# Attention of the prompt: score tiles over two PSUM banks, and GpSimd in the split of q and k and in the squares of the output

## The chip, the core and the metric

The kernel runs on one core of a Trainium2 chip. The core has five engines with an instruction queue each: PE (matrix products, with its weight loads shown as PEld), DVE (vector), ACT (scalar and activation functions), POOL (GpSimd) and SP (here it only issues DMAs). They work on SBUF, 128 partitions wide, and on PSUM, which has eight banks of 512 fp32 columns per partition; products land in PSUM. The metric is the device time of one execution in microseconds, as the median of several runs.

## The reference

One inference step of a decoder with two layers: gated linear attention, then differential attention, each followed by an MLP and layer norms. It treats a prompt of 1024 tokens after 16 meta tokens, and eight running sequences with one new token each. The change lies in the differential attention of the prompt, 8 heads, each with two maps of 64 dimensions and values of 128:

```python
def diff_core(q, k, v, q_pos, k_pos, lam):
    s = jnp.einsum('bqhmd,bkhmd->bhmqk', q, k).astype(F32) * (DIFF_DH ** -0.5)
    mask = k_pos[None, :] <= q_pos[:, None]
    s = jnp.where(mask, s, -jnp.inf)
    p = jax.nn.softmax(s, axis=-1)
    a = p[:, :, 0] - lam * p[:, :, 1]
    return jnp.einsum('bhqk,bkhe->bqhe', a, v.astype(F32))

def diff_output(o, g_sub, lam_init, w_out, dtype):
    B, T = o.shape[:2]
    o = rms_norm(o, g_sub) * (1.0 - lam_init)
    return o.reshape(B, T, DIFF_HEADS * DIFF_DV).astype(dtype) @ w_out
```

So per head: scores of both maps, causal mask, two softmaxes, their weighted difference times the values, and a root-mean-square norm over the 128 values of a head, for which the squares of the output are summed.

## The kernel before

The kernel is one long function, `hybrid_step`. Instructions are written in program order in a tile framework. A planner puts them on the engines in an order of its own, worked out with modelled times, and inserts the waits; each engine then runs its queue strictly in that order. Tiles come from pools: a pool with `bufs=3` has three places for a name, and a fourth tile of that name waits until the first is free. PSUM is shared out for the whole kernel as three banks `mm` (products), three `ax` (transposes and small things) and two `sm` (long accumulations).

Products of fp32 accuracy are made of fp32r parts: `split` (L159 to L161) casts a tile to its high part on ACT (L160) and subtracts that from the tile on DVE (L161), which leaves the low part.

The attention stage (L1036 to L1198) runs over 8 heads and, in each, over 8 query tiles t of 128 rows.

- `prep(h)` (L1054) loads k, q and v of a head from DRAM, transposes k and q on PE through `ax` banks, four blocks of 128 at a time (L1077, L1082, L1087), and splits them into the tiles XH and XL (L160, L161). It writes into one half of XH and XL, head h + 1 while head h uses the other half. For heads 1 to 7 nine DMAs on POOL's queue (`move`, L1093 to L1099) then spread and copy parts over partitions, so that one product of 128 rows does the work of two of 64. Three of the moves (L1094 and twice L1099) overwrite what an earlier one reads, and wait on POOL for its landing. `prep(h + 1)` stands in program order ahead of the first tile of head h.
- `tile_(h, t, ...)` (L1102) has W = 16 + 128 (t + 1) keys. It cuts W into 1, 2 or 3 pieces of at most 512, and per map and piece makes the scores in one `mm` bank (L1117 to L1119 for head 0, L1121 and L1122 for the others). One DVE instruction (L1125, in the profile a custom operation and a read of its accumulator) scales the piece by -0.125, adds the mask, writes it to SBUF (`as`) and leaves the running minimum of the row. The first piece of a row starts from a constant, the later ones from the minimum so far. Then ACT makes the exponentials and their sums (L1127), DVE the weights (L1129, L1130) and the difference of the maps (L1131), PE transposes it (L1140), ACT copies that to SBUF (L1142), and PE multiplies by the values into the output bank `po`, an `sm` bank (L1145).
- After every fourth tile ACT copies the output bank to Y (L1180), squares it in place (L1181), and DVE sums the squares (L1182).
- After every second head `o_norm` scales the heads on POOL (a power in L1156, a multiply of 128x2048 in L1157). The last head is scaled in two parts on DVE, and `o_fm` transposes the result into XH and XL for the output projection.

The mask tile `cm` (`cmask`) has 448 columns: zeros, and the causal triangle in the last 128.

Of the kernel before, what the change touches and what calls it, by code (L numbers as in the profile page):

```python
# [88 lines left out]
def hybrid_step(ctx, tc, A, dbg=None, upto=9):  # L89
# [10 lines left out]
    mm = ctx.enter_context(tc.tile_pool(name="mm", bufs=3, space=PSUM))  # L100
    ax = ctx.enter_context(tc.tile_pool(name="ax", bufs=3, space=PSUM))
    sm = ctx.enter_context(tc.tile_pool(name="sm", bufs=2, space=PSUM))

    def mmt():
        return mm.tile([P, 512], F32, name="mmt")

    def axt():
        return ax.tile([P, 512], F32, name="axt")

    def smt():  # L110
        return sm.tile([P, 512], F32, name="smt")

    def cload(name, pool=cp):
        a, b = CCOL[name]
# [939 lines left out]
    def prep(h):  # L1054
# [22 lines left out]
        TE.transpose(ps[:, :NM], km, ident[:NM, :NM])  # L1077
        split(kh_[:, :NM], kl_[:, :NM], ps[:, :NM])
        for c in range(2):
            ps = axt()  # L1080
            for i in range(4):
                TE.transpose(ps[:, i * P : (i + 1) * P], kx[:, 4 * c + i, :], ident)  # L1082
            cs = slice(NM + 512 * c, NM + 512 * c + 512)
            split(kh_[:, cs], kl_[:, cs], ps)
            ps = axt()
            for i in range(4):
                TE.transpose(ps[:, i * P : (i + 1) * P], qx[:, 4 * c + i, :], ident)  # L1087
            cs = slice(512 * c, 512 * c + 512)
            split(qh_[:, cs], ql_[:, cs], ps)
        if h == 0:  # L1090
            return vm, vx, kh_, qh_, ql_, kl_
        move = nc.gpsimd.dma_start
# [8 lines left out]

    def tile_(h, t, out, vm, vx, k2, q2, ql2, kl_):  # L1102
        W = NM + P * (t + 1)
        nch = -(-W // 512)
        step = -(-W // nch // 16) * 16
        cuts = [(x, min(x + step, W)) for x in range(0, W, step)]
        sc_ = scp.tile([P, 2, NM + T], F32, name="as")
        st = a3.tile([P, 2, 2], F32, name="ast")
        mns, neg = st[:, 0, :], st[:, 1, :]
        l = ls[:, t, h, :]  # L1110
        ts_ = slice(t * P, (t + 1) * P)
        for m in range(2):
            r = slice(64 * m, 64 * m + 64)
            for ci, (x, y) in enumerate(cuts):
                ps = mmt()[:, : y - x]
                if h == 0:
                    TE.matmul(ps, q2[r, ts_], k2[r, x:y], start=True, stop=False)  # L1117
                    TE.matmul(ps, q2[r, ts_], kl_[r, x:y], start=False, stop=False)
                    TE.matmul(ps, ql2[r, ts_], k2[r, x:y], start=False, stop=True)  # L1119
                else:  # L1120
                    TE.matmul(ps, q2[m][:, ts_], k2[m][:, x:y], start=True, stop=False)  # L1121
                    TE.matmul(ps, ql2[m][:, ts_], k2[m][:, x:y], start=False, stop=True)  # L1122
                w = y - x
                mk = cm[:, CW - w :] if y == W else cm[:, 0:1].broadcast_to([P, w])
                V.tensor_tensor_reduce(sc_[:, m, x:y], ps, mk, -0.125, -NEG if ci == 0 else mns[:, m : m + 1], ALU.add, ALU.min, mns[:, m : m + 1])  # L1125
        for m in range(2):
            S.activation(sc_[:, m, :W], sc_[:, m, :W], AF.Exp, bias=mns[:, m : m + 1], scale=-1.0, accum_out=l[:, m : m + 1])  # L1127
# [3 lines left out]
        V.scalar_tensor_tensor(sc_[:, 0, :W], sc_[:, 1, :W], neg[:, 0:1], sc_[:, 0, :W], ALU.mult, ALU.add)  # L1131

        keys = [(0, vm)] + [(NM + j * P, vx[:, j, :]) for j in range(t + 1)]
        ats = []
        for j0 in range(0, t + 2, 4):
            n = min(4, t + 2 - j0)
            ps = axt()
            for j in range(n):
                x = keys[j0 + j][0]
                TE.transpose(ps[:, j * P : (j + 1) * P], sc_[:, 0, x : x + P], ident)  # L1140
            at = a3.tile([P, 4, P], F32, name="aT")
            S.copy(at[:, :n, :].rearrange("p j q -> p (j q)"), ps[:, : n * P])  # L1142
            ats += [at[:, j, :] for j in range(n)]
        for j, (at, (x, v)) in enumerate(zip(ats, keys)):
            TE.matmul(out, at, v, start=j == 0, stop=j == t + 1)  # L1145
# [23 lines left out]
    for h in range(8):  # L1169
        head = nxt  # L1170
        for n, t in enumerate((3, 2, 1, 0, 7, 6, 5, 4) if h == 7 else (7, 1, 5, 3, 6, 0, 4, 2)):
# [6 lines left out]
            if n % 4 == 3:  # L1178
                ts = (slice(0, 4), slice(4, 8))[n // 4] if h == 7 else slice(t % 2, 8, 2)
                S.copy(Yd[:, ts, h], po.rearrange("p (t e) -> p t e", e=P))  # L1180
# [139 lines left out]
```

## Time and profile before

| | |
|---|---|
| median of 3 runs | 2976.41 us (2976.1 to 2979.01) |
| profiled execution, whole | 2971.24 us |
| its span in the profile | 2969.5 us |
| granted TensorE clock, mean | 0.989 |
| PE busy | 2871.7 us, 97% |
| PE weight loads busy | 2321.0 us, 78% |
| DVE busy | 1578.4 us, 53% |
| ACT busy | 944.4 us, 32% |
| POOL busy | 846.2 us, 28% |
| chain that ended last, by engine | PE 79%, DVE 8%, DMA 7% |

The profile is of one execution. Busy times are unions over the engine's instructions; records of matmuls overlap, so a busy PE isn't a PE at its peak. Averages over the span mix stages with different limits: the first two thirds and the last quarter are weight products, and the attention of the prompt lies between, from about 1823 us to about 2090 us of the span. In a row of a timeline, the first number is the start, the second the duration, and a bracket at the end tells how long the engine was idle before and what ended that. In a row of a group, the count follows the shapes; then come busy microseconds and the mean of one in nanoseconds, and after that idle time before.

### The profile page before, as it was taken

To read this page: it belongs to the slowest core of one execution; us is meant where nothing else is said; L and a number is where in the kernel's file an instruction comes from. 1 tells how busy PE (TensorE), PEld (TensorE's weight loads), DVE (VectorE), ACT (ScalarE), POOL (GpSimd) and SP (SyncE) were. 2 spreads that over 40 slices of the span, in tenths; PEclk is the share of its full clock that TensorE was granted. 3 is DMA by queue.
4 is the path that set the end of the run, shared out by engine and by line. 5 is a ranking of instruction groups with operands and counts; after the bars stand their busy time and mean duration, and the time that the engine had idled before them with its cause. 6 is when DMAs were issued, how large, how long until landed. Compare 5 with 4: busy or idle time off the path is not lost.

```text
span 2969.5 us, 50730 instructions
## 1 busy us (share of the span) xinstructions
PE 2871.7 (97%) x19476; PEld 2321.0 (78%) x19476; DVE 1578.4 (53%) x2713; ACT 944.4 (32%) x1970; POOL 846.2 (28%) x605
## 2 busy tenths in 40 slices
PE   8999999999999999999989999999999999999998
PEld 5766668987767667666788887888998889888886
DVE  2563544468777766776777722889452212211115
ACT  2343344152122122122321113778242232223322
POOL 1322122234333433433323320223312222222224
PEclk9999999999999999999999999999999999999999
DMA  8667551525798887989588988564411111111111
GB/s 275 192 205 239 177 176 38 180 84 161 272 322 302 284 312 266 348 290 316 197 270 292 355 292 228 108 124 106 167 33 56 50 42 34 57 43 47 37 38 65
DMA packets 265730, 525.55 MB, mean 177 GB/s; under 512 B 30528, under 2 KB 162368, under 8 KB 261392
## 3 DMA queue, kind: packets, MB, share of 16 engines
q1 hardware_dynamic: 260448, 505.71, 50.9%
q0 software_dynamic: 5040, 16.61, 2.8%
q8 instruction: 153, 2.51, 0.4%
q14 instruction: 89, 0.73, 0.1%
HBM read 479.65 MB, written 25.99 MB: 170 GB/s over the span
## 4 chain that ended last, share of the span: by engine, by line
PE 79%; DVE 8%; DMA 7%; issue 2%; POOL 1%; ACT 1%; SPq 1%; DVEq 0%; POOLq 0%; ACTq 0%
PE mmt L164 22%; PE mmt L166 22%; PE mmt L165 22%; PE smt L776 4%; PE smt L1145 2%; DVE pg L735 1%; DVE as L1125 1%; DMA pg<-in_cache_v 1%; PE smt L953 1%; DMA swt<-in_mlp_w 1%; PE smt L417 1%; PE axt L1140 1%; DVE sc L736 1%; PE axt L891 1%; DVE as L1131 1%
## 5 line engine op out<-in xcount | busy, mean ns | idle before, releaser
L152 POOL TENSOR_TENSOR wlo<-raw,whi 128x512 fp32r<-128x512 f32 x384 | 528.7, 1393 | 1375.9 <-ACT whi L151 1220.9
L164 PE MATMUL mmt<-XH,whi 128*128 128x512 f32 (+1 forms) x1536 | 555.6, 362 | 5.8 <-DVE HL L161 5.8
L166 PE MATMUL mmt<-XH,wlo 128*128 128x512 f32 (+1 forms) x1536 | 554.4, 361 | 0.0
L165 PE MATMUL mmt<-XL,whi 128*128 128x512 f32 (+1 forms) x1536 | 553.6, 361 | 0.0
L151 ACT CAST whi<-raw 128x512 fp32r<-128x512 f32 x384 | 227.5, 619 | 931.1 <-PE mmt L166 492.6
L164 PE MATMUL mmt<-whi,XH 128*128 128x256 f32 x1536 | 440.5, 288 | 7.4 <-ACT Y L561 3.9
L165 PE MATMUL mmt<-wlo,XH 128*128 128x256 f32 x1536 | 437.7, 286 | 0.8 <-POOL wlo L152 0.8
L166 PE MATMUL mmt<-whi,XL 128*128 128x256 f32 x1536 | 437.3, 285 | 0.0
L164 PE MATMUL mmt<-whi,HH 128*128 128x512 f32 x1024 | 411.2, 402 | 1.4 <-DVE Y L962 1.4
L166 PE MATMUL mmt<-whi,HL 128*128 128x512 f32 x1024 | 407.7, 398 | 0.0
L165 PE MATMUL mmt<-wlo,HH 128*128 128x512 f32 x1024 | 407.4, 398 | 0.0
L736 DVE TENSOR_REDUCE sc<-pg 128x16 f32<-128x1024 f32 x256 | 308.9, 1213 | 86.5 <-POOL pg L735 83.8
L962 DVE TENSOR_TENSOR Y<-Y,mmt 128x512 f32<-128x512 f32 x256 | 174.9, 684 | 326.9 <-PE mmt L166 326.3
L164 PEld LDWEIGHTS mmt<-XH,whi 128*128 128x128 f32 x1536 | 290.0, 189 | 47.5 <-issue 10.1
L165 PEld LDWEIGHTS mmt<-XL,whi 128*128 128x128 f32 x1536 | 289.7, 189 | 46.7 <-issue 15.6
L166 PEld LDWEIGHTS mmt<-XH,wlo 128*128 128x128 f32 x1536 | 289.9, 189 | 44.7 <-issue 12.6
L164 PEld LDWEIGHTS mmt<-whi,XH 128*128 128x128 f32 x1536 | 290.5, 189 | 32.8 <-issue 22.9
L165 PEld LDWEIGHTS mmt<-wlo,XH 128*128 128x128 f32 x1536 | 290.8, 189 | 17.4 <-issue 15.4
L166 PEld LDWEIGHTS mmt<-whi,XL 128*128 128x128 f32 x1536 | 290.7, 190 | 10.3 <-issue 9.7
L735 DVE TENSOR_TENSOR pg<-pg,qb 128x1024 f32<-128x1024 f32 x192 | 264.5, 1383 | 36.3 <-DMA pg<-in_cache_k 29.6
L161 DVE TENSOR_TENSOR HL<-mmt,HH 128x344 fp32r<-128x344 f32 (+1 forms) x160 | 93.1, 583 | 351.9 <-ACT HH L160 351.8
L164 PEld LDWEIGHTS mmt<-whi,HH 128*128 128x128 f32 x1024 | 192.9, 188 | 74.4 <-issue 16.5
(371 smaller groups left out, 3623.2 us busy)
## 6 DMA issues: line engine op xcount, KB each, us to landing
pg<-in_cache_k SPq DMA_DIRECT2D x256, 512.0 KB
pg<-in_cache_v SPq DMA_DIRECT2D x256, 512.0 KB
raw<-in_mlp_w SPq DMA_DIRECT2D x256, 256.0 KB
swt<-in_mlp_w SPq DMA_DIRECT2D x32, 1024.0 KB
raw<-in_gla_w_in SPq DMA_DIRECT2D x48, 256.0 KB
swt<-in_gla_w_in SPq DMA_DIRECT2D x12, 1024.0 KB
swt<-in_diff_w_in SPq DMA_DIRECT2D x12, 1024.0 KB
raw<-in_diff_w_in SPq DMA_DIRECT2D x48, 256.0 KB
```

The source lines that it names most:

```text
L151: S.copy(hi[:, c], raw)
L152: G.tensor_tensor(lo[:, c], raw, hi[:, c].bitcast(F32), op=ALU.subtract)
L161: return eng.tensor_tensor(lo, src, hi.bitcast(F32), op=ALU.subtract)
L164: TE.matmul(ps, ah, bh, start=first, stop=False)
L165: TE.matmul(ps, ah, bl, start=False, stop=False)
L166: TE.matmul(ps, al, bh, start=False, stop=last)
L417: TE.matmul(ps[o : o + TS, :], lhs[:, k + i, :], t[:, i, c * 512 : (c + 1) * 512], start=k == 0, stop=k == nk - 2)
L735: eng.tensor_tensor(pg, pg, qb, op=ALU.mult)
L736: V.tensor_reduce(sc[:, n, :], pg.rearrange("p (h d) -> p h d", d=64), op=ALU.add, axis=AX.X)
L776: TE.matmul(acc[i * TS : i * TS + 16, :256], w[r, n, :], pg[r, i * 256 : (i + 1) * 256], start=n == 0, stop=n == NPG)
L962: steps_v.append(V.tensor_tensor(yv, yv, ps, op=ALU.add).ins)
L1145: TE.matmul(out, at, v, start=j == 0, stop=j == t + 1)
```

## The change

Three things are changed in the stage.

1. The PSUM banks are shared out anew for the stage: two buffers `sc` of two banks each for scores, three `ax`, and one `sm` in place of two. Before and after the stage the old shares hold. A row of W scores is cut into 1, 2 or 4 equal pieces of at most 512; up to two pieces lie in the two banks of one `sc` buffer, and one L1125 takes both. The mask tile grows to 912 columns for that.
2. For heads 1 to 7, k and q are not split by ACT and DVE out of PSUM. ACT copies the transposed 128x512 to SBUF (`fm`, two buffers), GpSimd copies it to the high part and subtracts for the low part. Head 0, and the 16 meta columns of k, are split as before.
3. The squares of the output are made by GpSimd from Y in SBUF into a tile `o2`, in place of ACT's square in the bank; DVE sums `o2`.

```diff
@@
+    banks = {}
+
+    def psum(**bufs):
+        if banks:
+            banks.pop("all").close()
+        e = banks["all"] = ExitStack()
+        for n, b in bufs.items():
+            banks[n] = e.enter_context(tc.tile_pool(name=n, bufs=b, space=PSUM))
+
+    ctx.callback(lambda: banks["all"].close())
+    psum(mm=3, ax=3, sm=2)
...
     de.close()
+    psum(sc=2, ax=3, sm=1)
...
+    a4 = e.enter_context(tc.tile_pool(name="a4", bufs=2))
     scp = e.enter_context(tc.tile_pool(name="scp", bufs=5))
-    CW = 448
+    CW = 912
...
+            for x, hi, lo, o in ((kx, kh_, kl_, NM), (qx, qh_, ql_, 0)):
+                ps = axt()
+                for i in range(4):
+                    TE.transpose(ps[:, i * P : (i + 1) * P], x[:, 4 * c + i, :], ident)
+                cs = slice(o + 512 * c, o + 512 * c + 512)
+                if h == 0:
+                    split(hi[:, cs], lo[:, cs], ps)
+                    continue
+
+                f = a4.tile([P, 512], F32, name="fm")
+                S.copy(f, ps)
+                G.tensor_copy(hi[:, cs], f)
+                G.tensor_tensor(lo[:, cs], f, hi[:, cs].bitcast(F32), op=ALU.subtract)
...
-        nch = -(-W // 512)
-        step = -(-W // nch // 16) * 16
-        cuts = [(x, min(x + step, W)) for x in range(0, W, step)]
+        nch = (1, 2, 4)[(W > 512) + (W > 1024)]
+        n = W // nch
...
-            for ci, (x, y) in enumerate(cuts):
-                ps = mmt()[:, : y - x]
...
-                V.tensor_tensor_reduce(sc_[:, m, x:y], ps, mk, -0.125, -NEG if ci == 0 else mns[:, m : m + 1], ALU.add, ALU.min, mns[:, m : m + 1])
+            for c in range(0, nch, 2):
+                k = min(nch, 2)
+                pss = banks["sc"].tile([P, 2, 512], F32, name="sct")[:, :k, :n]
+                for i in range(k):
+                    x, ps = (c + i) * n, pss[:, i, :]
+                    y = x + n
...
+                w, x = k * n, c * n
+                mk = cm[:, CW - w :] if x + w == W else cm[:, 0:1].broadcast_to([P, w])
+                f = lambda a: a.rearrange("p (i n) -> p i n", i=k)
+                V.tensor_tensor_reduce(f(sc_[:, m, x : x + w]), pss, f(mk), -0.125, -NEG if c == 0 else mns[:, m : m + 1], ALU.add, ALU.min, mns[:, m : m + 1])
...
-                S.activation(po, po, AF.Square)
-                V.tensor_reduce(oss[:, ts, h], po.rearrange("p (t e) -> p t e", e=P), op=ALU.add, axis=AX.X)
+                o2 = a4.tile([P, 4, P], F32, name="o2")
+                G.tensor_tensor(o2, Yd[:, ts, h], Yd[:, ts, h], op=ALU.mult)
+                V.tensor_reduce(oss[:, ts, h], o2, op=ALU.add, axis=AX.X)
...
     e.close()
+    psum(mm=3, ax=3, sm=2)
```

The functions `mmt`, `axt` and `smt` take their tiles from the share that holds at the time.

More of the change, by code (lines that the diff above doesn't have):

```diff
@@ L99, in hybrid_step @@
     wrp = ctx.enter_context(tc.tile_pool(name="wrp", bufs=2))
-    mm = ctx.enter_context(tc.tile_pool(name="mm", bufs=3, space=PSUM))
-    ax = ctx.enter_context(tc.tile_pool(name="ax", bufs=3, space=PSUM))
-    sm = ctx.enter_context(tc.tile_pool(name="sm", bufs=2, space=PSUM))
+    banks = {}
[7 more added lines that the diff above has]
+    psum(mm=3, ax=3, sm=2)
     def mmt():
-        return mm.tile([P, 512], F32, name="mmt")
+        return banks["mm"].tile([P, 512], F32, name="mmt")
     def axt():
-        return ax.tile([P, 512], F32, name="axt")
+        return banks["ax"].tile([P, 512], F32, name="axt")
     def smt():
-        return sm.tile([P, 512], F32, name="smt")
+        return banks["sm"].tile([P, 512], F32, name="smt")
     def cload(name, pool=cp):
```

26 lines of the change are left out of this document (7 added, 19 removed).

## The prediction

> **What bounds the kernel now.** I read the page first for the span, then the whole change lies in one stage, attention of the prompt, so I cut that stage by head in the table of windows (each row from one head's first score matmul to the next one's), and after it the chain of waits, the list of waits, and the timeline around head switches.
>
> ```profile
> span 2969.5 us, 50730 instructions
> ```
>
> ```profile
> core 0: us, PE busy (x) PEld busy (x) DVE busy (x) ACT busy (x) POOL busy (x), PEclk, DMA share, GB/s
> 1860.00:1888.00 28.00, 26.54 (x202) 24.55 (x200) 25.73 (x91) 22.93 (x57) 4.58 (x9) 1.00 0.63 134
> 1888.00:1921.00 33.00, 29.08 (x209) 25.97 (x209) 29.25 (x91) 22.44 (x56) 11.14 (x11) 0.98 0.61 128
> 1921.00:1953.00 32.00, 29.60 (x196) 27.05 (x197) 24.67 (x81) 21.39 (x51) 4.58 (x9) 0.86 0.64 125
> 1953.00:1987.00 34.00, 29.99 (x221) 27.36 (x220) 28.11 (x98) 27.06 (x67) 8.80 (x11) 0.96 0.55 115
> 1987.00:2014.00 27.00, 26.31 (x181) 24.18 (x180) 22.27 (x79) 18.17 (x44) 7.01 (x10) 0.92 0.49 112
> 2014.00:2043.00 29.00, 28.25 (x226) 27.20 (x224) 28.17 (x93) 25.24 (x63) 10.95 (x11) 1.00 0.44 102
> 2043.00:2087.00 44.00, 39.10 (x308) 36.16 (x307) 36.14 (x107) 32.72 (x73) 10.62 (x8) 1.00 0.27 83
> sum 261.00, PE 240.30 PEld 217.77 DVE 217.57 ACT 189.25 POOL 62.48; mean PE 30.04 PEld 27.22 DVE 27.20 ACT 23.66 POOL 7.81
> ```
>
> The stage is taken as 1826 to 2087 us, 261 us of 2969.5. In each row the numbers after the window's length are busy times of PE, weight loads, DVE, ACT and POOL. DVE is full or nearly so in three heads (25.73 of 28, 29.25 of 33, 28.17 of 29) and at 77 to 83% in the other rows. POOL is busy for 62.48 of 261 us, mostly issuing and waiting. PE shows 240.30, but matmul records overlap one another, so that is not a floor. The chain for the same stretch:
>
> ```profile
> by line: PE smt L1145 17.6%; DVE as L1125 14.7%; issue 10.6%; PE axt L1140 8.7%; DVE as L1131 7.4%; DMA XL<-XL 5.0%; PE mmt L1121 4.7%; PE mmt L1122 4.6%; ACT as L1127 4.0%; DMA ht<-in_ln_mix_g 2.9%; DVE XL L161 2.7%; DMA XH<-XH 2.6%; DMA w
> ```
>
> No engine owns it. PE's lines (L1145, L1140, L1121, L1122) hold 36%, the DVE lines that the change touches (L1125 14.7%, L1131 7.4%, L161 2.7%) 25%, and the copies that spread q and k over partitions (XL<-XL, XH<-XH) 7.6%. So work taken from DVE comes back only in part. The third kind of limit shows at the head switches:
>
> ```profile
> 1886.87 0.51 POOL L1099 DMA_DIRECT2D XL<-XL  x1 [2.83 <-DMA XL<-XL]
> 1888.43 0.40 PE L1121 MATMUL mmt<-XH 128*128 128x352 f32 x1 [1.16 <-DMA XH<-XH]
> ...
> 1947.14 0.51 POOL L1099 DMA_DIRECT2D XL<-XL  x1 [2.65 <-DMA XL<-XL]
> 1954.14 0.41 PE L1121 MATMUL mmt<-XH 128*128 128x352 f32 x1
> ...
> 1985.55 0.63 PE L1121 MATMUL mmt<-XH 128*128 128x352 f32 x1 [3.65 <-DMA XH<-XH]
> ```
>
> The fourth and fifth numbers of such a row are the work; the bracket is idle time and what ended it. Head 2 begins (1888.43) when the copies that POOL issued last have landed, and head 5 waits 3.65 us for them. Head 4 begins 7 us after its last copy was issued. So two of the six switches from head 1 on hang on the preparation of the next head, and it is this preparation that the change puts on POOL.
>
> **Part 1, one minimum for two banks.** Per head and map, the tiles t = 0 to 7 took 1, 1, 1, 2, 2, 2, 2, 3 minimums, 14 in all; now they take one each and t = 7 two, 9 in all. Over 16 pairs of head and map that is 224 down to 144. All 80 removed are of the kind that starts from the running minimum, of which there are 96 now and 16 after:
>
> ```profile
> L1125 DVE CUSTOM_DVE_ANT_0 as<-mmt,cmask,ast x96: 470/568/684, 1829.4 to 2073.4; 128x352 f32<-128x352 f32 x16, 128x336 f32<-128x336 f32 x16, 128x384 f32<-128x384 f32 x16, 128x256 f32<-128x256 f32 x16
> ```
>
> ```profile
> L1125 DVE CUSTOM_DVE_ANT_0 as<-mmt,cmask 128x400 f32<-128x400 f32 x32 | 17.7, 566 | 1.4 <-PE mmt L1122 1.1 <-PE mmt L1119 0.4
> L1125 DVE CUSTOM_DVE_ANT_0 as<-mmt,cmask 128x272 f32<-128x272 f32 x32 | 13.8, 436 | 1.3 <-PE mmt L1122 1.2
> ```
>
> ```profile
> 1900.58 0.61 DVE L1125 CUSTOM_DVE_ANT_0 as<-mmt,cmask,ast 128x384 f32<-128x384 f32 x1
> 1901.12 0.08 DVE L1125 DVE_READ_ACCUMULATOR2_ANT ast<- 128x1 f32 x1
> ...
> 1901.28 0.67 DVE L161 TENSOR_TENSOR XL<-axt,XH 128x512 fp32r<-128x512 f32 x1
> 1901.86 0.61 DVE L1125 CUSTOM_DVE_ANT_0 as<-mmt,cmask,ast 128x384 f32<-128x384 f32 x1
> ```
>
> The columns stay, so an instruction saves its fixed part. From the two shapes a column costs (566-436)/128 = 1.02 ns. The chained one of 384 columns starts at 1900.58 and the next instruction at 1901.12 (its read of the accumulator is in that): 0.54 - 384 x 0.00102 = 0.15 us fixed. 80 x 0.15 = 12.0 us off DVE. If a two-bank operand cost something per bank, no row shows it; the bounds are 12.0 and, at the whole mean of the longer read, 0.
>
> PE gets more instructions: t = 7 goes from three chunks to four, 2 x (7 x 2 + 3) = 34 matmuls and weight loads. The columns are the same, so the cost is between 0 and 34 loads; the last row of the windows gives 217.77 us of loads over some 1700 of them, 0.13 us each, 4.4 us at most. I take +1, since loads run beside matmuls. Against it, PE waits for score banks:
>
> ```profile
> POOL XH L1099 <- DMA XH<-XH: 18.0, 5, 7.2
> POOL XL L1099 <- DMA XL<-XL: 15.9, 6, 4.2
> PEld mmt L1121 <- DVE ast L1125: 11.9, 22, 2.5
> ```
>
> The third row (11.9 us in 22 waits) is PE held by a bank that DVE hasn't emptied. Two buffers of two banks hold a longer piece than three of one bank for the wide tiles and fewer pieces for the narrow ones: between -11.9 and a few us more. I take -1.
>
> The output bank `smt` goes from two buffers to one, so the next group's first product must wait for the copy of the last group:
>
> ```profile
> 1900.56 0.59 ACT L1180 COPY Y<-smt 128x512 f32<-128x512 f32 x1 [1.02 <-PE smt L1145]
> ```
>
> ```profile
> 1906.05 0.39 PE L1145 MATMUL smt<-vm,aT 128*128 128x128 f32 x2
> ```
>
> The copy ends at 1901.15 and the next group starts at 1906.05: 4.9 us of cover, in which PE transposes and scores. I cost it at nothing; if the cover went, a copy (0.59 us) would show 16 times, 9 us.
>
> The new layouts of the banks at both ends of the stage can hold back the out-projection's first matmuls, which run inside the last window. PE has 44 - 39.10 = 4.9 us free there, which is the upper bound; I take 0, because the scores end before the output tiles do.
>
> **Part 2, the split of q and k for heads 1 to 7.** On ACT a copy takes the place of the cast of the same 128x512 (cost 0). On DVE 28 subtracts go; the timeline above has one at 1901.28 and its successor at 1901.86: 28 x 0.58 = 16.2 us. On POOL come 28 subtracts, 28 copies, and from part 3 16 squares:
>
> ```profile
> L1157 POOL TENSOR_TENSOR Y<-Y,orr 128x2048 f32<-128x2048 f32 x3 | 10.9, 3621 | 0.0
> L152 POOL TENSOR_TENSOR wlo<-raw,whi 128x512 fp32r<-128x512 f32 x6 | 7.7, 1290 | 25.4 <-ACT whi L151 12.8 <-PE axt L1163 12.6
> ```
>
> ```profile
> L781 POOL MEMSET pg<- 128x256 f32 x8 | 2.5, 307 | 3.2 <-DVE sc L736 2.4 <-PE smt L776 0.8
> ```
>
> A subtract of this very shape takes 1.29 us: 36.1. A square reads two operands as well: 20.6 (at least 3.62/4 = 0.91 us each by the wide multiply, 14.5). A copy with one input has no row. It lies between twice the memset of 256 columns, 0.61 us, and the subtract; I take 0.7, nearer to the first since it has one operand less to fetch than the second: 19.6 (17.1 to 36.1). In all 76 us (68 to 93) on an engine with 198 us free.
>
> What it delays is the move. Now L1093 leaves 0.3 us after the cast of the last piece of k:
>
> ```profile
> 1902.96 0.58 ACT L160 CAST XH<-axt 128x512 fp32r<-128x512 f32 x1
> 1903.83 0.51 POOL L1093 DMA_DIRECT2D XH<-XH  x1 [16.45 <-ACT XH L160]
> ```
>
> The cast ends at 1903.54. POOL's copy has to come between, +0.7 us at least. A subtract of the piece before it or a square of the head before may still run: with half a subtract 1.35 us late, with a whole subtract and a whole square 3.3. Next in line is the first score matmul of the next head, at the switches that already hang on it. Two at 1.35 give 2.7; the bounds are 0 (the planner starts the preparation earlier) and six switches x 3.3 = 20. I take +3.
>
> **Part 3, the squares.** ACT loses 16 squares of the output bank. It is busy for 189 of 261 us (last row of the windows) and its 4.0% of the chain is the exponential (L1127), which stays; I give the squares no credit. The sum on DVE reads the same number of elements, but now waits for POOL, and behind it on DVE stand minimums for which PE and ACT wait. POOL stands still behind landings for 18.0 + 15.9 = 33.9 us in 11 waits (the first two rows of waits). That is 13% of the stage, so 2 of 16 squares meet one, for half of 3.1 us: 3 us on DVE. Bounds: 0, and 16 x 3.1 = 50 if the planner were wrong each time.
>
> **The port.** Both engines use SBUF:
>
> ```profile
> 1913.73 5.12 DVE L1131 SCALAR_TENSOR_TENSOR as<-as,ast 128x912 f32<-128x912 f32 x2
> ```
>
> ```profile
> 1915.05 3.62 POOL L1157 TENSOR_TENSOR Y<-Y,orr 128x2048 f32<-128x2048 f32 x1
> ```
>
> ```profile
> L1131 DVE SCALAR_TENSOR_TENSOR as<-as,ast 128x144 f32<-128x144 f32 x8 | 9.2, 1146 | 0.0
> ```
>
> ```profile
> L1131 DVE SCALAR_TENSOR_TENSOR as<-as,ast x64: 358/894/4043, 1837.2 to 2078.6; 128x1040 f32<-128x1040 f32 x8, 128x272 f32<-128x272 f32 x8, 128x784 f32<-128x784 f32 x8, 128x528 f32<-128x528 f32 x8
> ```
>
> The second of two L1131 in the first row took 4.04 us (the maximum of the last row) and ended as POOL's 3.62 us multiply ended. The narrow form's mean of 1.146 us against a least of 0.358 makes 8 x 0.79 = 6.3 us lost beside 10.9 us of such multiplies, 0.58 per us. The new POOL instructions are short (76/72 = 1.06 us), so one hit costs about half of that: 64 starts of L1131 x 76/261 = 19 hits x 0.53 = 10 us. Bounds: 0, if the planner's order keeps them apart, and 0.58 x 76 = 44.
> [...]
>
> **The sum.** DVE: -12.0 - 16.2 + 3 + 10 = -15.2 us. How much reaches the end has two ends. By the chain, L1125's 14.7% is 38 us, and the part saved is 12.0 of 96 x 0.568 + 128 x about 0.51 = 120 us, so 3.8; L161's 2.7% is 7.0 us, 28 of 32 of it 6.2; L1131's 7.4% is 19.3 us, and 10 more on 64 x 0.894 = 57 makes 3.4; the 3 us of waiting at DVE's quarter is 0.8. That gives -5.8. Were DVE full throughout, it would be -15.2. The middle, -10.4, fits a stage whose heads are half full of DVE. With +3 for the moves, +1 for PE and -1 for banks: -7.4, say -8 us. The profiled execution took 2971.2 us in all (span 2969.5 and 1.7 around it), which becomes 2963.2. The runs shown have a median of 2976.41, 5.2 us above it, so against these I say 2968.4.
>
> **Rivals.** (A) Slower: the preparation becomes the bound at each switch. One mechanism: POOL works eight pieces, 4 x 1.99 = 8 us, in the queue ahead of the nine moves, and head h + 1 starts when they land. For it: two switches hang on landings now, and POOL takes its queue in order, with DMA waits in it. Against it: head 4's 7 us of slack, and casts that come one after another, so that POOL can work on the first while ACT makes the next. It decides once the moves come over 3 us later: six switches x 3.3 = 20, less the 8 that DVE gives outside of them: +12, 2988. (B) Faster than I say: DVE is the bound in nearly all heads, its saving comes through whole and the preparation starts earlier with it: -28.2 + 8 = -20, 2956. For it: the rows at 89 to 97%; against it: PE's 36% of the chain. (C) The port at its rate for long multiplies: DVE -28.2 + 3 + 44 = +19, at a quarter (its share of the chain) +5: 2981. (D) The change does its work but PE's order and the landings pace the heads: 28 us of DVE go into idle time, -1, 2975. For it: DVE at 77 to 83% in four of seven rows.
>
> **The numbers.** Forecast 0.40 (own range 2961 to 2975), A 0.20, B 0.26, C 0.08, D 0.06. 0.2% is 6.0 us, about what this measurement can tell from no change. Faster by that: 0.28 of the forecast and all of B, 0.54. Slower: 0.16 of A and 0.04 of C, 0.20. The rest, 0.26, is within. The range reaches from B's far side to the middle of A, 2953 to 2988, and leaves out about 0.16.
>
> **What would show it.** Right: 144 minimums, 16 of them chained; 28 subtracts on POOL near 1.3 us; the stage 5 to 12 us shorter, most of it in rows that had DVE at 89% and more; the first score matmul of a head waiting for landings no longer than now. The copy's row on POOL prices the one unknown duration. The port is right if L1131's total rises by about 10 us, wrong if its rows keep to their least times or if it rises by 40. Wrong altogether: head starts that follow the landings of the copies by nothing at all six switches (A), the sum over squares on DVE showing long waits for POOL, or the DVE rows falling to 70% with the heads as long as before (D).

## The result, and the profile after

The changed kernel takes 2996.46 us (median of 6 runs, 2988.78 to 3005.58), the kernel before in the same session 2978.8 us (6 runs): ratio 1.0062, 95% interval 1.0043 to 1.0082. It is slower by some 18 us, where 8 us less were forecast. The executions of the changed kernel form two groups, 2989 to 2992 us at a mean granted clock of 0.985 to 0.988 and 3001 to 3006 us at 0.981 to 0.982; the profile below is of the first (2988.78 us), so it shows about 18 us over the profile of before (2971.2 us).

The page's first line, and the table of windows cut by head as before (window and its length, then busy times of PE, weight loads, DVE, ACT and POOL, then the granted clock, DMA share and GB/s):

```profile
span 2986.7 us, 50669 instructions
```

```profile
1824.00:1856.00 32.00, 29.76 (x207) 25.26 (x208) 22.62 (x59) 20.37 (x48) 14.09 (x18) 1.00 0.74 175
1856.00:1888.00 32.00, 31.64 (x256) 30.09 (x255) 24.71 (x71) 25.07 (x62) 16.67 (x20) 1.00 0.52 121
1888.00:1921.00 33.00, 27.50 (x208) 25.20 (x207) 25.25 (x64) 21.45 (x53) 21.62 (x21) 1.00 0.55 125
1921.00:1948.00 27.00, 24.00 (x180) 21.89 (x179) 23.27 (x63) 20.35 (x50) 14.76 (x19) 1.00 0.66 148
1948.00:1993.00 45.00, 33.61 (x251) 31.23 (x250) 28.24 (x67) 25.76 (x61) 27.78 (x29) 0.91 0.43 101
1993.00:2017.00 24.00, 23.20 (x143) 21.22 (x144) 18.92 (x54) 16.21 (x40) 5.90 (x11) 0.81 0.49 100
2017.00:2063.00 46.00, 34.48 (x261) 32.78 (x262) 29.39 (x76) 27.49 (x67) 29.13 (x27) 0.90 0.34 75
2063.00:2106.00 43.00, 40.35 (x272) 37.53 (x272) 28.56 (x75) 27.56 (x61) 6.28 (x6) 0.83 0.29 87
sum 282.00, PE 244.55 PEld 225.20 DVE 200.96 ACT 184.26 POOL 136.24; mean PE 30.57 PEld 28.15 DVE 25.12 ACT 23.03 POOL 17.03
```

The eight rows make 282 us against 261. The loss lies within them: from the last score to the end of the span the changed kernel took 898.3 us, the kernel before 899.8. DVE did lose work, 217.57 to 200.96 us, and POOL gained 74. The heads changed very unevenly: heads 1 to 3 took 92 us (93 before), head 4 took 45 (34) and head 6 took 46 (29). In these two PE was idle for 11.4 and 11.5 us, against 4.0 and 0.8 before. Both windows end at a switch of heads, and there PE stands still. The timeline of PE at the switch to head 5 (its transposes, L1094, already belong to head 6):

```profile
1984.85 1.47 PE L1094 MATMUL axt<-c_ident,wlo 128*128 128x128 f32 x12
1992.82 0.77 PE L1139 MATMUL sct<-XH 128*128 128x260 f32 x2 [6.50 <-POOL XH L1102]
```

The first score of head 5 (L1139, the old L1121) came after 6.50 us of idle PE, that of head 7 after 9.49 us, 16.0 us together. Before, the switches to heads 2 and 5 waited 1.16 and 3.65 us, and the one to head 7 not at all. The row names a cast of POOL as what ended the wait, but that cast is one of head 6. What landed 0.1 us ahead of this product, at 1992.73 us, was the eighth of head 5's moves (L1113, issued at 1985.41, 7.3 us to its landing). The eighth move of head 7, issued at 2057.23, landed 5.2 us later at 2062.46, and its first score came at 2062.60. So PE waited for moves at both switches. What POOL did in the 20 us ahead of head 7, as the timeline of POOL shows it (L1102 and L1103 are the new cast and subtract, L1175 and L1176 the power and multiply of `o_norm`, L1201 the new square, L161 the split of a weight tile, L1107 to L1113 the nine moves):

```profile
2031.50 2.92 POOL L1175 TENSOR_TENSOR orr<-orr,mhalf 128x16 f32<-128x16 f32 x1 [0.98 <-DVE orr L1174]
2034.40 1.27 POOL L1103 TENSOR_TENSOR XL<-fm,XH 128x512 fp32r<-128x512 f32 x1
2035.63 1.08 POOL L1102 CAST XH<-fm 128x512 fp32r<-128x512 f32 x1
2036.67 3.61 POOL L1176 TENSOR_TENSOR Y<-Y,orr 128x2048 f32<-128x2048 f32 x1
2040.23 1.49 POOL L1102 CAST XH<-fm 128x512 fp32r<-128x512 f32 x1
2041.68 1.28 POOL L1103 TENSOR_TENSOR XL<-fm,XH 128x512 fp32r<-128x512 f32 x1
2042.90 0.61 POOL L1107 DMA_DIRECT2D XH<-XH  x1
2047.97 1.03 POOL L1201 TENSOR_TENSOR o<-Y 128x512 f32<-128x512 f32 x1 [4.46 <-ACT Y L1199]
2048.97 1.25 POOL L1103 TENSOR_TENSOR XL<-fm,XH 128x512 fp32r<-128x512 f32 x1
2050.18 0.57 POOL L1111 DMA_DIRECT2D XH<-XH  x1
...
2053.81 1.03 POOL L1201 TENSOR_TENSOR o<-Y 128x512 f32<-128x512 f32 x1 [0.51 <-ACT Y L1199]
2054.81 2.47 POOL L161 TENSOR_TENSOR wlo<-raw,whi 128x512 fp32r<-128x512 f32 x2
2057.23 0.58 POOL L1113 DMA_DIRECT2D XH<-XH  x1
2060.01 0.51 POOL L1113 DMA_DIRECT2D XL<-XL  x1 [2.20 <-DMA XL<-XL]
```

No single row is long. The queue is taken in order: the first move stands behind splits and 6.5 us of scaling; then a square waits 4.46 us for ACT's copy of the output, with a subtract and six moves behind it; and the eighth move stands behind a square and two weight splits. From the first move to the last 17 us pass. Head 5's moves are spread from 1964.50 to 1988.69, and one wait in there is for the head after it: the first cast of head 6 stands ahead of head 5's eighth move, and waits for ACT's copy.

```profile
1984.86 0.61 POOL L1102 CAST XH<-fm 128x512 fp32r<-128x512 f32 x1 [6.01 <-ACT fm L1101]
```

The nine moves were never close together. In the kernel before they are spread over 11 to 17 us a head too, since some of them wait for landings: 16.8 us for head 5 and 11.0 us for head 7, where the multiply of the scaling stood behind the last move:

```profile
2028.83 0.51 POOL L1093 DMA_DIRECT2D XH<-XH  x1 [17.36 <-ACT XH L160]
2039.82 0.51 POOL L1099 DMA_DIRECT2D XL<-XL  x1 [1.87 <-DMA XL<-XL]
2040.35 3.62 POOL L1157 TENSOR_TENSOR Y<-Y,orr 128x2048 f32<-128x2048 f32 x1
```

So the change lengthened the spread by 7.4 us for head 5 and by 6.1 us for head 7, and not for the others (10 to 14 us, before 11 to 17). The eighth moves of these two heads also took 7.3 and 5.2 us to land, where they took 3.2 and 2.9 us before; why is not known.

What POOL's new work cost, and what became of DVE's (groups by line; count, busy us and mean ns of one, then idle time ahead of them), and a row of the list of waits (total us, times, longest):

```profile
L1103 POOL TENSOR_TENSOR XL<-fm,XH 128x512 fp32r<-128x512 f32 x28 | 37.8, 1354 | 0.1
L1102 POOL CAST XH<-fm 128x512 fp32r<-128x512 f32 x28 | 20.5, 737 | 55.5 <-ACT fm L1101 55.3
L1201 POOL TENSOR_TENSOR o<-Y 128x512 f32<-128x512 f32 x16 | 17.2, 1077 | 63.6 <-ACT Y L1199 63.6
```

```profile
L1144 DVE DVE_READ_ACCUMULATOR2_ANT ast<- 128x1 f32 x144 | 11.8, 82 | 0.0
L1150 DVE SCALAR_TENSOR_TENSOR as<-as,ast 128x1040 f32<-128x1040 f32 (+5 forms) x64 | 67.0, 1046 | 1.2
```

```profile
DVE oss L1202 <- POOL o L1201: 12.8, 4, 5.2
```

144 minimums remain. The difference of the maps (L1150, the old L1131) rose to 67.0 us; the same 64 took 60.7 us before. The chain of waits for the stage:

```profile
by line: PE smt L1164 16.9%; DVE as L1144 9.6%; PE axt L1159 8.8%; issue 8.7%; PE sct L1139 7.2%; PE sct L1140 6.3%; DVE as L1150 5.3%; DMA XL<-XL 5.1%; ACT as L1146 3.3%; DMA raw<-in_mlp_w 2.6%; PE axt L1094 2.5%; POOL XL L1103 2.3%; DMA X
```

The minimums fell from 14.7% to 9.6% and the difference of the maps from 7.4% to 5.3%; POOL's subtract (2.3%) is new on the chain, and the landings of XL are still there.

### The profile page after: what moved, and what is told of

Read it like the earlier page. It is cut to its first block, busy times and chain, and to the rows that moved or that the text cites. A ratio compares the mean times of both kernels' runs of the same rounds, so it can differ in the third digit from the quotient of the medians.

```text
span 2986.7 us, 50669 instructions
## 1 busy us (share of the span) xinstructions
PE 2877.5 (96%) x19510; PEld 2328.6 (78%) x19510; DVE 1564.5 (52%) x2525; ACT 936.5 (31%) x1954; POOL 923.1 (31%) x677
## 4 chain that ended last, share of the span: by engine, by line
PE 82%; DMA 6%; DVE 6%; POOL 2%; issue 1%; ACT 1%; SPq 1%; DVEq 0%; POOLq 0%; ACTq 0%
PE mmt L173 22%; PE mmt L175 22%; PE mmt L174 22%; PE smt L785 4%; PE smt L1164 2%; PE smt L962 1%; DVE pg L744 1%; DVE as L1144 1%; DMA pg<-in_cache_v 1%; PE smt L426 1%; PE axt L1159 1%; DMA swt<-in_mlp_w 1%; PE axt L900 1%; PE sct L1139 1%; DMA swt<-vs 1%
## 5 line engine op out<-in xcount | busy, mean ns | idle before, releaser
L161 POOL TENSOR_TENSOR wlo<-raw,whi 128x512 fp32r<-128x512 f32 x384 | 531.7, 1401 | 1350.0 <-ACT whi L160 1206.4
L173 PE MATMUL mmt<-XH,whi 128*128 128x512 f32 (+1 forms) x1536 | 555.6, 362 | 6.1 <-DVE HL L170 6.1
L173 PE MATMUL mmt<-whi,XH 128*128 128x256 f32 x1536 | 441.8, 288 | 5.1 <-ACT Y L570 3.7
L173 PE MATMUL mmt<-whi,HH 128*128 128x512 f32 x1024 | 410.6, 401 | 1.5 <-DVE Y L971 1.5
L173 PEld LDWEIGHTS mmt<-XH,whi 128*128 128x128 f32 x1536 | 289.9, 189 | 47.8 <-issue 9.3
L173 PEld LDWEIGHTS mmt<-whi,XH 128*128 128x128 f32 x1536 | 291.5, 190 | 31.3 <-issue 23.2
L175 PEld LDWEIGHTS mmt<-whi,XL 128*128 128x128 f32 x1536 | 291.6, 190 | 11.5 <-issue 10.1
L173 PEld LDWEIGHTS mmt<-whi,HH 128*128 128x128 f32 x1024 | 192.6, 188 | 74.3 <-issue 16.9
```

The lines of the kernel that those rows point to most:

```text
L161: G.tensor_tensor(lo[:, c], raw, hi[:, c].bitcast(F32), op=ALU.subtract)
L173: TE.matmul(ps, ah, bh, start=first, stop=False)
L175: TE.matmul(ps, al, bh, start=False, stop=last)
```

## The experiments

All ratios are to the kernel before, timed in the same session on the same chip, with 95% intervals; 0.001 is 3 us. Three theories were set up: Q, POOL's queue holds the moves back; S, the new shares of PSUM lose by themselves; P, DVE is held while POOL works (the expectations put it down to a port, which no run shows). H came later: the new shares of PSUM hold PE up at the start of the stage and its granted clock falls there (in head 0 it was 0.69 in e1, 0.85 before). Every edit lets the planner order the stage anew, and no run separates that from the edit itself. The new lines shift the line numbers of every kernel; the operations and names stay.

### The parts of the change alone

```diff
 e1: only the scores; split and squares on ACT and DVE
-                f = a4.tile([P, 512], F32, name="fm")
-                S.copy(f, ps)
-                G.tensor_copy(hi[:, cs], f)
-                G.tensor_tensor(lo[:, cs], f, hi[:, cs].bitcast(F32), op=ALU.subtract)
+                split(hi[:, cs], lo[:, cs], ps)
-                G.tensor_tensor(o2, Yd[:, ts, h], Yd[:, ts, h], op=ALU.mult)
+                S.activation(o2, Yd[:, ts, h], AF.Square)
 e2: the second of these edits alone; e3: the first alone
 e4: the kernel before, with the fm, G.tensor_copy, G.tensor_tensor lines in place of split
```

> Changed kernel with the split of heads 1 to 7 back on ACT and DVE, and the squares made by ACT from Y into the same SBUF tile; only the two-bank scores and the new shares of PSUM stay. Theory Q (the time is lost in POOL's queue, where splits, squares and scaling stand ahead of the moves of the next head): with the new POOL work gone the loss is gone, and the 80 minimums saved show: 0.995 to 0.999 of before, 2964 to 2976 us. Rival S (the new shares of PSUM lose it, one output bank and two score buffers): still 1.004 or more. Rival P (DVE held at the port by POOL): as Q, since POOL's new work is gone; L1131's total back to about 61 us.

> Changed kernel with the squares alone taken from POOL: ACT makes them from Y into the same tile. Q: the waits of POOL for the copy of the output (63.6 us in 15 waits, with moves queued behind) are gone, but the splits stay ahead of the moves: half of the loss or more comes back, 0.998 to 1.003 of before, and the starts of heads 5 and 7 wait less than 6.5 and 9.5 us. P: 17 of 75 us of POOL's new work go, so a quarter of 6 us on DVE: 1.005 to 1.006. S: 1.006.

> Changed kernel with the split back on ACT and DVE for all heads; squares stay on POOL. Q: the moves no longer wait for POOL's own copies, but squares that wait for ACT may still stand ahead of them: 0.996 to 1.002 of before. P: most of POOL's new work is gone: 0.999 to 1.001. S: 1.006.

> Kernel before with the split of heads 1 to 7 on POOL alone; scores, banks and squares as before. Q: the preparation of each head gets longer on POOL by some 4 to 8 us and head starts wait for landings: 1.001 to 1.006 of before. S: no loss, and DVE's 16 us saved show: 0.995 to 0.998. P: 1.000 to 1.002 by collisions, with no longer waits at head starts.

Measured: e1 2982.34 us, 1.0023 (1.0009 to 1.0037); e2 2985.74, 1.0028 (1.0013 to 1.0043); e3 2986.25, 1.0030 (1.0015 to 1.0046); e4 2992.75, 1.0053 (1.0037 to 1.0069). No part wins, and the parts don't add up. By the expectations, e2 and e4 fit Q; e1 and e3 came out above Q's ranges and below S's 1.004 and 1.006. The split alone (e4) shows the same pattern as the whole change, late at the switches to the same two heads, 5 and 7:

```profile
2000.28 0.93 PE L1125 MATMUL mmt<-XH 128*128 128x352 f32 x2 [5.19 <-POOL XH L1092]
2071.01 1.00 PE L1125 MATMUL mmt<-XH 128*128 128x272 f32 x3 [8.46 <-DMA XH<-XH]
```

With the new scores beside it (e2) the planner found an order with smaller gaps (PE waits 4.8 us for landings, 3.6 of them at head 7), so the delay isn't a fixed price of an instruction. In e1, with no new work on POOL, the list of waits between heads 1 and 7 shows PE waiting for landings too, here at the second product of a head's first scores (0.9 us before):

```profile
PE sct L1133 <- DMA XL<-XL: 9.5, 5, 2.3
```

And in e2 the wait of DVE's sum for the squares is there although ACT makes them, so the 12.8 us in 4 waits of the changed kernel are no proof against POOL:

```profile
DVE oss L1202 <- ACT o L1201: 12.0, 4, 5.6
```

### The moves out of POOL's queue

```diff
 e6 (from the changed kernel), e9 (before), e10 (e1), e11 (e2), e16 (e4), e17 (e3)
-        move = nc.gpsimd.dma_start
+        move = lambda a, b: nc.sync.dma_start(a.bitcast(F32), b.bitcast(F32))
```

> The changed kernel with one edit: the nine moves of a head are issued on SP's queue and no longer on POOL's. Theory Q (what is late is the moves, since splits, squares, the power and the scaling stand ahead of them on POOL): the waits of 6.5 us ahead of head 5 and 9.5 us ahead of head 7 fall to less than 3 us each, and 10 to 15 us come back: ratio to before 1.001 to 1.003. Theory P (DVE is held at the port while POOL works) and theory H (new shares of PSUM and the clock): the waits for landings may fall, but the time does not, ratio 1.005 to 1.006.

> The kernel before with one edit: the nine moves of a head are issued on SP's queue. It is the control for e6_moves_on_sp. If the 13 us that e6 won come from the queue that the change filled (theory Q), the kernel before, whose POOL has little else ahead of the moves and PE waits 5.7 us for their landings between heads 1 and 7, wins 4 us at most: ratio 0.9985 to 1.000. If SP is the better queue whatever stands on POOL, it wins as much as e6 did: ratio 0.995 to 0.997.

> Only the two-bank minimum and the new PSUM shares (as e1_scores_only), with the moves on SP's queue. In e1's profile PE waited 9.5 us in 5 waits for the last move ahead of the second product of a head's first scores (0.9 us before). Theory Q, taken further (the saving on DVE is given back at the landings of the moves, even without any new work on POOL): these waits fall under 4 us and the ratio is 0.996 to 0.999. Theory S (the new shares of PSUM lose by themselves, at the start of the stage and for one output bank): the ratio stays at 1.002.

> Scores and split as in the changed kernel, squares on ACT, moves on SP's queue. With e10 and e6 it prices the POOL work apart from the moves. Theory P (DVE is held while POOL reads SBUF; in e6 the difference of the maps took 56.2 us between heads 1 and 7, 45.9 before, and PE's transposes waited 8.6 us for it, 2.4 before): the split's 52 us of POOL work cost 4 to 8 us over e10 although they take 16 us of subtracts from DVE, ratio to before 1.000 to 1.002. Without P the subtracts taken from DVE show: 3 to 6 us below e10.

> The kernel before, its banks and its scores, with only the split of heads 1 to 7 on POOL and the moves on SP's queue. With e4_split_only (1.0053, moves on POOL) it tells what the split costs by its place in POOL's queue. Theory Q: 14 us or more come back, ratio 0.996 to 1.000, since 16 us of subtracts leave DVE. Theory P (the port eats what the subtracts gave): 1.000 to 1.002.

> Scores and squares as in the changed kernel, the split on ACT and DVE again, moves on SP's queue. e6 and e11 differ by the squares on POOL alone, by 0.0046. If the squares lose because they stand in one queue with the split's casts (and wait there for ACT's copy of the output, 89.6 us in 14 waits in e6, with casts behind), then without the split on POOL they cost nothing: the ratio of e10, 0.999 to 1.001. If squares on POOL lose by themselves (DVE's sum waits for them, or the port), the ratio is 1.003 to 1.005.

| parts of the change | moves on POOL | moves on SP | difference |
|---|---|---|---|
| none | 1 | e9 0.9991 (0.9982 to 1.0001) | 0.0009 |
| scores | e1 1.0023 | e10 0.9999 (0.9990 to 1.0008) | 0.0024 |
| split | e4 1.0053 | e16 0.9997 (0.9985 to 1.0009) | 0.0056 |
| scores, squares | e3 1.0030 | e17 1.0020 (1.0007 to 1.0034) | 0.0010 |
| scores, split | e2 1.0028 | e11 0.9976 (0.9960 to 0.9993) | 0.0052 |
| all | 1.0062 | e6 1.0022 (1.0010 to 1.0034) | 0.0040 |

With the same work on POOL, taking the nine moves past it is worth 12 us for the whole change, 17 us for the split alone and 15 us for scores and split, but 7, 3 and 3 us where no split stands on POOL. A difference of two ratios is itself uncertain by some 0.002, 6 us, so the latter three are hardly more than noise and the first three are clear of it. That is theory Q. For two of the three the traces show how it is won: the late switches of the changed kernel and of e4 are gone in e6 and e16. In e6 the list of waits for the stage has, in place of 16 us,

```profile
PE sct L1139 <- DMA XH<-XH: 2.0, 1, 2.0
PE sct L1140 <- DMA XL<-XL: 1.6, 1, 1.6
```

In e16 such waits come to 2.1 us, where e4 has the 5.2 and 8.5 us above. For the others it is not shown. In e2 only 4.8 us of such waits could go, and e11 is 15 us better. In e10 the waits were expected to fall under 4 us, and they did not:

```profile
PE sct L1133 <- DMA XL<-XL: 9.7, 5, 3.2
```

So e10 took less time than e1 for another reason, which wasn't found.

These moves only copy bits; in eight kernels here (e6, e9, e10, e11 and e15 to e18) they are issued from SP, with both sides named float32.

e11, the change without its squares and with its moves on SP, beats the kernel before: 2975.43 against 2979.32 us, 7 us by the ratio. Theory P, by which the split's POOL work would cost 4 to 8 us over e10, failed; it wins 7, give or take 6.

The squares stay a loss: 0.0046 (14 us) between e11 and e6, 0.0034 between e2 and the changed kernel, 0.0021 between e10 and e17, and 0.0007 between e1 and e3, which is within the noise. By the expectation of e17 they should have cost nothing without the split beside them, or as much as with it; they cost about half (the interval of e17 is 4 us to either side). In e6 the squares waited for ACT's copy with casts behind them:

```profile
POOL o L1201 <- ACT Y L1199: 89.6, 14, 18.4
```

in e17 DVE waits 0.8 us for them in the whole stage, and what it loses there isn't found.

### The shares of PSUM

```diff
 e12 and e13: the kernel before, its PSUM shared out anew for the stage only
 ...
+    psum(mm=4, ax=3, sm=1)
+    psum(mm=3, ax=3, sm=1)
 e5 (from the changed kernel), e8 (from e1)
-    psum(sc=2, ax=3, sm=1)
+    psum(ax=3, sc=2, sm=1)
 e14 (from the changed kernel), e15 (from e11)
-    psum(sc=2, ax=3, sm=1)
+    psum(sc=2, ax=2, sm=2)
```

> The kernel before with only its PSUM shared out anew for the stage: four product banks, three for transposes and one for the output in place of three, three and two; scores, splits and squares as before. Theory S: the one output bank and the new layout at the ends of the stage cost what e1_scores_only lost, 5 to 7 us: ratio 1.002. Otherwise (the prediction costed the output bank at nothing, with a cover of 4.9 us): within 0.001 of 1.

> The kernel before with one output bank in place of two during the stage (three product banks, three for transposes, one for the output; one bank unused). If the one output bank is what cost e12_banks_only its 7 us, the ratio is 1.002 to 1.003 again and ACT's copy of the output waits some 17 us for its last product (5.7 us before); if it was the fourth product bank or the new layout, the ratio is within 0.001 of 1.

e12 2986.98 us, 1.0024 (1.0012 to 1.0036); e13 2979.24 us, 1.0014 (1.0004 to 1.0024). One output bank in place of two costs 4 us with nothing else changed (3 us is the half-width of the interval), and 7 with the layout of e12, which is not clear of e13. In the one trace of e12, of 2995.77 us, between heads 1 and 7, ACT waits for the last product of a group ahead of its copy, and landings come late behind it:

```profile
ACT Y L1190 <- PE smt L1155: 17.1, 6, 6.6
PE mmt L1131 <- DMA XH<-XH: 14.8, 4, 4.7
```

In e13 the first of these is 3.6 us, against the 17 that were expected, and no wait stands out. That the one output bank loses is shown by the edit; by which wait, or by which order of the planner, is not.

> The changed kernel with one edit: the three transpose banks (ax) are the first in the new share of PSUM, so they lie on the three old product banks, and the score buffers come behind them. Theory H (the start of the stage under the new shares makes PE idle and its granted clock falls to half in head 0): in the changed kernel the first transposes of the stage lie on banks that the running sequences' last work still holds, and the first score waits for it. With the edit head 0 begins some 2 us sooner, no stretch at half clock lies in head 0, and the runs that took 3001 to 3006 us are gone: 7 us less than the changed kernel, ratio to before about 1.004. Heads 5 and 7 still start 6 and 9 us late. Theory Q (POOL's queue holds the moves at the switches to heads 5 and 7): no change, ratio 1.006.

> The kernel with only the two-bank minimum and the new PSUM shares (splits on ACT and DVE, squares on ACT, as in e1_scores_only), with the three transpose banks first in the share. Theory H: head 0 has no stretch at half clock, 5 to 7 us less than e1_scores_only, ratio to before 1.000 or just below it (0.998 to 1.0005). Theory S (the shares lose by their number, one output bank and two score buffers): the ratio stays at 1.002.

e5 3002.3 us, 1.0098 (1.0078 to 1.0118); e8 2994.95, 1.0068 (1.0045 to 1.0092), 13 us over e1. Theory H fell: the other order of banks gave nothing back in head 0 (e5 34 us at a clock of 1.00, the changed kernel 32 at 1.00; e8 39 us at 0.74, e1 38 at 0.69), and heads 5 and 7 of e5 still wait 5.1 and 9.4 us. It lost at the end: from the last score to the end of the span e5 takes 906.9 us and e8 910.8, where the changed kernel takes 898.3 and e1 898.5. The same 20 us behind the attention, windows and timeline of PE, first of e1, then of e8:

```profile
2103.00:2123.00 20.00, 18.75 (x162) 18.61 (x161) 9.12 (x17) 8.47 (x14) 6.11 (x5) 1.00 0.95 326
```

```profile
2105.21 0.36 PE L173 MATMUL mmt<-whi,XH 128*128 128x256 f32 x1
...
2114.02 0.60 PE L1175 MATMUL axt<-c_ident,Y 128*128 128x128 f32 x4
```

```profile
2100.00:2120.00 20.00, 15.25 (x97) 13.91 (x96) 7.67 (x15) 8.71 (x15) 11.88 (x4) 0.74 0.91 315
```

```profile
2109.69 1.09 PE L1175 MATMUL axt<-c_ident,Y 128*128 128x128 f32 x4 [1.27 <-DVE Y L1169]
...
2112.34 0.58 PE L173 MATMUL mmt<-whi,XH 128*128 128x256 f32 x1 [1.20 <-DVE XL L1177]
```

e1 issues 162 products and transposes there and e8 97, with PE idle for 4.75 us and at a clock of 0.74. When the old shares return, the product banks of the next stage take the first three banks. With scores there, they have long been free, and the first product of the output projection (L173, 2105.21 us) runs ahead of the last `o_fm` transposes (L1175, 2114.02). With transposes there, it has to wait for the last of them: 2112.34 behind 2109.69. The row names DVE's XL as what it waited for; this product doesn't read XL, but DVE reads the bank of those transposes to make it.

> The changed kernel with PSUM shared as two score buffers of two banks, two transpose banks and two output banks. Theory S: two output banks give back 5 to 7 us, ratio 1.003 to 1.004, with the waits for landings at heads 5 and 7 still there (theory Q). If the third transpose bank mattered as much, ratio 1.006 or more.

> As e11_split_moves_on_sp, with two transpose banks and two output banks. Theory S: 5 to 7 us faster than e11, ratio to before 0.995 to 0.9965. If the third transpose bank mattered as much, the ratio is 0.998 or above.

e14 3004.75 us, 1.0097 (1.0079 to 1.0115); e15 2997.95 us, 1.0081 (1.0063 to 1.0098), which is 0.0105 or 31 us over e11. e14 is 10 us over the changed kernel, give or take 8. The output bank's 4 us were bought with a transpose bank that is worth more. The wait of the scores' weight loads for DVE between heads 1 and 7, e11 and then e15:

```profile
PEld sct L1139 <- DVE ast L1144: 6.7, 13, 0.7
```

```profile
PEld sct L1139 <- DVE ast L1144: 18.2, 26, 2.2
```

That is 11.5 us of the 31, and 5.6 us more lie behind the last score (904.8 us to the end, against 899.2 in e11); the rest was not followed up.

### Two edits that told little

```diff
 e7 (from the changed kernel): the scaling is written four tiles later
-        if h < 6 and h % 2:
-            o_norm(G, slice(0, 8), slice(h - 1, h + 1))
+            if n == 4 and h in (2, 4, 6):
+                o_norm(G, slice(0, 8), slice(h - 2, h))
 ...
 e18 (from e11)
+    a5 = e.enter_context(tc.tile_pool(name="a5", bufs=4))
-                f = a4.tile([P, 512], F32, name="fm")
+                f = a5.tile([P, 512], F32, name="fm")
```

> The changed kernel with one edit: the scaling of two finished heads on POOL (the power and the multiply of 128x2048, 6.5 us together) is written four tiles later, behind the nine moves of the next head's preparation and no longer ahead of them. Within theory Q this tells the long POOL work from the short: if the scaling is what makes heads 5 and 7 late, their waits of 6.5 and 9.5 us fall below 3 us and 8 to 12 us come back, ratio to before 1.002 to 1.004; if the splits and squares alone are enough, the waits stay within 2 us of what they were and the ratio is 1.006.

> e11_split_moves_on_sp with four buffers fm in place of two, so that ACT's copies of the next head's k and q never wait for POOL's subtract. In e11 neither ACT's nor PE's waits on that side were large (PE's transposes waited 1.9 us for fm), so theory Q expects no more than 2 us: ratio 0.9965 to 0.998. If the two buffers pace the preparation, 0.995 or less.

e7 2995.43 us, 1.0078 (1.0059 to 1.0098). The planner put the scaling where it was, ahead of the moves, and the waits for heads 5 and 7 are 5.3 and 9.5 us again. It says nothing on the scaling; it is nearly a repeat of the changed kernel, with the same result within the intervals. e18 2972.7 us, 0.9987 (0.9974 to 1.0000), above the 0.9965 to 0.998 that were expected: no gain over e11 that the intervals show, so two buffers between ACT and POOL are enough.

## Why the prediction was wrong

**What held.** POOL's prices: 1.354 us a subtract (1.29 forecast), 0.737 a cast (0.7), 1.077 a square (1.29), 75.5 us in all (76). DVE's saving: its busy time in the stage fell by 16.6 us; the forecast without the wait of 3 us was -18.2. DVE beside POOL, which the prediction calls the port (no run shows by what DVE is held): the difference of the maps took 67.0 us in the changed kernel and, with no new POOL work, 59.6 in e10, so 7.4 us where 10 were forecast and 44 would have followed from the long multiplies:

```profile
L1143 DVE SCALAR_TENSOR_TENSOR as<-as,ast 128x1040 f32<-128x1040 f32 (+5 forms) x64 | 59.6, 935 | 0.7
```

POOL had longer rows there too: casts with a median of 0.612 us took 1.08 and 1.49 us in the timeline ahead of head 7, each begun while a difference of the maps was running on DVE (1.13 us from 2035.11, 3.72 us from 2037.53).

**The step that failed: "Two at 1.35 give 2.7 [...] I take +3" for the moves.** Two switches were hit, as the step said, though not its two: head 2 began on time, heads 5 and 7 were late. The step counted what one cast, a subtract and perhaps a square put ahead of the first move. All nine moves are instructions in that queue, and each of the new rows can stand among them, with the scaling, the weight splits, and the waits of squares and of the next head's casts for ACT. So heads 5 and 7 had their nine spread over 24.2 and 17.1 us in place of 16.8 and 11.0, and PE waited 16.0 us for them in place of 4.8 us at all switches. Head 7 had little slack to lose: before, its last move landed at 2042.64, and its scores began at 2042.92. The moves' place in the queue cost 12 us in the whole change (e6) and 17 for the split alone (e4 against e16). The stated upper bound for it, 20 us, was right, and the value taken from inside the bounds was far too low. Rival A named the place and sign, 2988; but it isn't a fixed 3.3 us at each of six switches, it is 6.5 and 9.5 us at two.

**One output bank "at nothing".** The cover of 4.9 us was read at one hand-over. It isn't nothing: 4 us (e13), 7 with the layout of e12. The cost was looked for in the copy; where it does arise stays open. Against that, the hand-over of banks at the end was rightly put at 0 (898.3 us behind the last score against 899.8): it holds for the order that the change uses, and the other costs 12 us there (e8).

**The squares, +3.** The wait of DVE was 12.8 us, but e2 has it with squares on ACT; the edit itself cost 2 to 14 us by what else is on POOL (e3, e17, e6), by a way that isn't found. Its bounds, 0 to 50, hold.

**What reaches the end.** With the moves out of the way, DVE's saving may come through in part: e11 is 7 us faster than the kernel before, and 4.5 us faster than e9, give or take 6, with the one output bank's cost within both. That doesn't contradict the middle of -10.4, nor does it show it. So the sum failed by its losses: some 12 us of moves, 4 to 7 of banks and 10 of squares (1.0062 against e2's 1.0028), which overlap and aren't additive, in place of +3, 0 and +3.

**The rivals.** B, DVE as the bound in nearly all heads, did not come: DVE is busy for 63 to 86% of a window. C, the port at the rate of long multiplies, is out by the 7.4 us. D, heads paced by PE's order and the landings, is half right: e1 and e10 have the whole saving of the minimums, and neither is faster than the kernel before.

## What to carry to other kernels

Work given to an engine with room cost here what stood behind it in that engine's queue, the DMAs that it issues (PE waited 16.0 us for them at two switches): list every instruction of the queue from the first to the last transfer, waits included, and price the switch by how much later the last ones land than before, not by one instruction. A plain copy needn't be issued from the engine that computes; here, issued from SP, that one edit was worth 12 to 17 us with the split on that engine. Give up a PSUM bank only after trying it alone (one output bank cost 4 us in e13), and look at which banks the next stage takes over (12 us behind the last score in e8).

## What the hardware showed beside that

The granted clock was lower behind the two longest idle stretches of PE in the stage. Behind the 6.5 us of idle PE at head 5 and the 9.5 us at head 7 the windows of the next heads show 0.81 and 0.83, where before they had 0.92 and 1.00. Cut finer, the clock is 0.50 from 1993.0 to 2002.3 and from 2063 to 2074, and 1.00 from 2002.3 to 2017. What that cost is not shown: heads 5 and 7 took 24 and 43 us, where they took 27 and 44 before.

The clock was low even where PE's records cover nearly the whole stretch. In the two stretches at 0.50 they cover 8.64 of 9.3 us and 10.77 of 11.0. In head 0 it shows more plainly; of e15:

```profile
1829.40:1863.50 34.10, 33.24 (x131) 28.09 (x130) 16.42 (x41) 14.23 (x32) 8.31 (x8) 0.50 0.54 127
```

PE's records cover 33.24 of 34.1 us, and yet the clock is 0.50. Head 0 differs from kernel to kernel: its clock was 0.85 before, 0.69 in e1, and 1.00 in the changed kernel, which took 32 us for the head where e15 took 44. Head 0 is the one head with products of 64 rows instead of 128. They are not enough to keep the clock down, since the changed kernel's head 0 has them too; what does is open.
